# A convolution on one core: fp32 loads on SyncE with casts on ScalarE in place of casting loads on GpSimd

## The chip, the core and the metric

The kernel runs on one core of a Trainium2 chip. The metric is the device time of one execution in microseconds (us). The kernel before takes 126.02 us, the median of three runs (125.80 to 126.24).

A core has five engines with an instruction stream each: TensorE (PE in the profile, with its weight loads as PEld), VectorE (DVE), ScalarE (ACT), GpSimd (POOL) and SyncE (SP, which only issues transfers here). Sixteen DMA engines move data between HBM and the on-chip memory SBUF. SP, ACT and POOL can issue DMAs, each on a ring of its own (q1, q10 and q0 in the profile). A DMA issued by POOL may change the type on the way; here it reads fp32 and writes fp16.

## The reference: what is computed

A 3x3 convolution with padding 1: 16 images of 64 channels, 64x64 pixels, and 128 output channels, all in fp32.

```
batch, c_in, h, w, c_out = 16, 64, 64, 64, 128
x_pad = np.pad(x, ((0, 0), (0, 0), (1, 1), (1, 1)), mode='constant')
for b, co, ci, kh, kw:
    output[b, co] += weight[co, ci, kh, kw] * x_pad[b, ci, kh:kh+h, kw:kw+w]
```

The input has 16.78 MB, the output 33.55 MB.

## The kernel before

**The arithmetic.** Two output rows, 2j and 2j+1, are made together, with five products in place of six for each column kw of the filter. With w0, w1, w2 the filter's rows and s = x[2j] + x[2j+1], row 2j is w1 s + (w2 - w1) x[2j+1] + w0 x[2j-1], and row 2j+1 is w1 s + (w0 - w1) x[2j] + w2 x[2j+2]. The product w1 s is shared. The five weights lie in `Wt` as G1, G21, G0, G01 and G2; they are made at the start from `w_raw` by transposing matmuls (line 91), copies and subtractions (lines 98 to 110).

**The tiles.** The images are taken in eight pairs p = 0 to 7. Image 2p lies on partitions 0 to 63, image 2p+1 on 64 to 127, one channel to a partition. A pair has a tile `xs` of fp16 (128 x 64 x 64), a tile `ss` of the row sums s in fp16 (128 x 32 x 64), and two output tiles `ot`, one to an image (128 output channels x 64 x 64 in fp32, 16 KB to a partition).

**A pair's work.** It is cut into four blocks of 16 output rows (8 row pairs, line 144). A block is written (p, blk) below. For each, PE makes three groups of products in PSUM: U (G1 with `ss`, 6 matmuls), A (G21 and G0 with `xs`, 12 matmuls) and B (G01 and G2 with `xs`, 12 matmuls), always for both images. ACT copies U to `ut` in SBUF (line 188). DVE adds A and `ut` into the even rows of `ot` (line 196), and B and `ut` into the odd rows (line 199). PE has 30 matmuls to a block, 960 in all (line 174).

**The loads.** SP loads the weights and the pairs 0, 1 and 2 in fp32 (lines 41 to 47), into tiles of the pool that later holds the outputs. Their fp16 copies are made by casts on ACT and POOL (line 104; `later`, line 115, says at which block each piece of 16 rows is cast). The pairs 3 to 7 come by casting DMAs that POOL issues (line 60): pairs 3 and 4 at the start, pairs 5, 6 and 7 between POOL's sums in pair 1, the last two pairs in halves. These have no fp32 tile and no casts. POOL makes `ss` of the next pair in two pieces at the beginning of each pair (line 137), for pairs 1 and 2 from the fp32 tile, for the others from `xs`; DVE makes that of pair 0.

**The stores.** Pair 0's first image, and both images of pair 7, are stored in halves after blocks 1 and 3, all others whole after block 3. SP issues the stores of the first image of each pair (line 201), as soon as DVE's last add into it is done. The stores of the second image are held and issued by ACT at the next block, after that block's copies of U (line 191).

**Order.** Each engine runs its instructions in the order of the program; `keep` marks those whose order is fixed as written. A DMA waits on the engine that issues it, and then stands in that engine's ring, first in, first out. The output pool has 7 buffers, `xs` 8, `ss` 3, `ut` 4.

Of the kernel before, what the change touches and what calls it, by code (L numbers as in the profile page):

```python
# [8 lines left out]
F32 = mybir.dt.float32  # L9
F16 = mybir.dt.float16  # L10
# [3 lines left out]
def kernel(  # L14
# [6 lines left out]
    nc = tc.nc  # L21
    B, CI, H, W = x.shape
    CO = weight.shape[0]
    assert H == 64 and W == 64 and CI == 64 and CO == 128 and B % 2 == 0
    NP = B // 2
    RB = 8

    keep = tc.keep_in_program_order
    x_rows = x.rearrange("b c h w -> (b c) h w")
# [2 lines left out]

    const = ctx.enter_context(tc.tile_pool(name="const", bufs=1))
    psum = ctx.enter_context(tc.tile_pool(name="psum", bufs=8, space=bass.MemoryType.PSUM))
    xpool = ctx.enter_context(tc.tile_pool(name="xpool", bufs=8))
    opool = ctx.enter_context(tc.tile_pool(name="opool", bufs=7))
    spool = ctx.enter_context(tc.tile_pool(name="spool", bufs=3))
    upool = ctx.enter_context(tc.tile_pool(name="upool", bufs=4))

    w_raw = const.tile([CO, CI * 9], F32)  # L40
    nc.sync.dma_start(w_raw, w_flat)
    x0 = opool.tile([128, H, W], F32, tag="ot", name="x0")
    nc.sync.dma_start(x0, x_rows[0:128, :, :])
    x1 = opool.tile([128, H, W], F32, tag="ot", name="x1")
    nc.sync.dma_start(x1, x_rows[128:256, :, :])
    x2 = opool.tile([128, H, W], F32, tag="ot", name="x2")
    nc.sync.dma_start(x2, x_rows[256:384, :, :])
    raws = {1: x1, 2: x2}
    ident = const.tile([128, 128], F16)
    make_identity(nc, ident)  # L50
    w16 = const.tile([CO, CI * 9], F16)
    keep(nc.gpsimd.tensor_copy(w16, w_raw))  # L52

    xs = {p: xpool.tile([128, H, W], F16, tag="xs", name="xs") for p in range(3)}

    def load(p, rows):
        xs[p] = xpool.tile([128, H, W], F16, tag="xs", name="xs")
        for lo in range(0, H, rows):
            keep(
                nc.gpsimd.dma_start(  # L60
                    xs[p][:, lo : lo + rows, :],
                    x_rows[128 * p : 128 * p + 128, lo : lo + rows, :],
                )
            )

    ss = {}

    def sums(eng, p, src, lo, n):
        if p not in ss:
            ss[p] = spool.tile([128, H // 2, W], F16, tag="ss", name="ss")  # L70
        v = src.rearrange("p (j i) c -> p j i c", i=2)
        keep(
            eng.tensor_add(  # L73
                ss[p][:, lo : lo + n, :], v[:, lo : lo + n, 0, :], v[:, lo : lo + n, 1, :]
            )
        )
# [5 lines left out]
    def wrow(i):  # L82
        return Wt[:, i, :, :].rearrange("p t c -> p (t c)")

    wps = {}
    for kh in (1, 2, 0):
# [3 lines left out]
            for q in (0, 64):  # L90
                nc.tensor.matmul(wp[q : q + 64, k * CO : k * CO + CO], w16[:, t::9], ident)  # L91
        wps[kh] = wp[:, 0 : 3 * CO]
    blank = const.tile([128, 400], F32)
    keep(nc.vector.memset(blank, 0.0))  # L94
    warm = psum.tile([128, 512], F32, tag="acc", name="warm")
    for _ in range(3):
# [3 lines left out]
    keep(nc.vector.tensor_sub(wrow(G21), wps[2], wrow(G1)))  # L100
    keep(nc.vector.tensor_sub(wrow(G01), wps[0], wrow(G1)))  # L101

    def cast(copy, p, src, lo, hi):
        keep(copy(xs[p][:, lo:hi, :], src[:, lo:hi, :]))  # L104

    for lo in (RB, 2 * RB, 3 * RB):
        sums(nc.vector, 0, x0, lo, RB)
    cast(nc.scalar.copy, 0, x0, 0, 18)
    keep(nc.scalar.copy(wrow(G0), wps[0]))  # L109
    keep(nc.scalar.copy(wrow(G2), wps[2]))  # L110
    cast(nc.gpsimd.tensor_copy, 0, x0, 34, 50)
    cast(nc.gpsimd.tensor_copy, 0, x0, 50, 64)
    for p in (3, 4):
        load(p, H)
    later = {
        (0, 0): [(0, x0, 18, 34)],
        (0, 2): [(1, x1, 0, 16), (1, x1, 16, 32)],
        (0, 3): [(1, x1, 32, 48), (1, x1, 48, 64)],
    }
    later.update({(1, n): [(2, x2, 16 * n, 16 * n + 16)] for n in range(4)})  # L120

    held = []

    whole = {3: (0, 64)}
    halves = {1: (0, 32), 3: (32, 64)}
    cuts_of = [(halves, whole)] + [(whole, whole)] * (NP - 2) + [(halves, halves)]

    def store(eng, p, b2, ot, lo, hi):
        return eng.dma_start(
            out_rows[2 * p + b2, :, lo:hi, :],  # L130
            ot.rearrange("p j i c -> p (j i) c")[:, lo:hi, :],
        )

    for p in range(NP):
        if p + 1 < NP:
            for lo in (0, 16):
                sums(nc.gpsimd, p + 1, raws.get(p + 1, xs[p + 1]), lo, 16)
                if (p, lo) == (1, 16):
                    for q in range(5, NP):
                        load(q, H if q == 5 else H // 2)  # L140
        ots = [
            opool.tile([128, H // 2, 2, W], F32, tag="ot", name="ot") for _ in range(2)
        ]
        for blk in range(4):
            j0 = blk * RB

            def group(wi_rows):

                tiles = [
                    psum.tile([128, RB, W], F32, tag="acc", name="acc") for _ in range(2)  # L150
                ]
                n = 3 * len(wi_rows)
                i = 0
                for wi, off in wi_rows:
                    for kw in (1, 0, 2):
                        c_lo, c_hi = max(0, 1 - kw), min(W, W + 1 - kw)
                        for b2 in range(2):
                            p0 = 64 * b2
                            lo, hi = j0, j0 + RB
                            if off is None:  # L160
                                rhs = ss[p][p0 : p0 + 64, lo:hi, c_lo + kw - 1 : c_hi + kw - 1]
                            else:
                                while 2 * lo + off < 0:
                                    lo += 1
                                while 2 * (hi - 1) + off > H - 1:
                                    hi -= 1
                                first = 2 * lo + off
                                last = 2 * (hi - 1) + off
                                rhs = xs[p][
                                    p0 : p0 + 64,  # L170
                                    first : last + 1 : 2,
                                    c_lo + kw - 1 : c_hi + kw - 1,
                                ]
                            nc.tensor.matmul(  # L174
                                tiles[b2][:, lo - j0 : hi - j0, c_lo:c_hi],
                                Wt[p0 : p0 + 64, wi, kw, :],
                                rhs,
                                start=i == 0,
                                stop=i == n - 1,
                            )  # L180
                        i += 1
                return tiles

            U = group([(G1, None)])
            us = []
            for b2 in range(2):
                ut = upool.tile([128, RB, W], F32, tag="ut", name="ut")
                keep(nc.scalar.copy(ut, U[b2]))  # L188
                us.append(ut)
            while held and (p, blk) != (1, 0):  # L190
                keep(store(nc.scalar, *held.pop(0)))
            for piece in later.get((p, blk), ()):
                cast(nc.scalar.copy, *piece)
            A = group([(G21, 1), (G0, -1)])
            for b2 in range(2):
                nc.vector.tensor_add(ots[b2][:, j0 : j0 + RB, 0, :], A[b2], us[b2])  # L196
            Bt = group([(G01, 0), (G2, 2)])
            for b2 in range(2):
                nc.vector.tensor_add(ots[b2][:, j0 : j0 + RB, 1, :], Bt[b2], us[b2])  # L199
            if blk in cuts_of[p][0]:  # L200
                store(nc.sync, p, 0, ots[0], *cuts_of[p][0][blk])
            if blk in cuts_of[p][1]:
                held.append((p, 1, ots[1], *cuts_of[p][1][blk]))
    while held:
        keep(store(nc.scalar, *held.pop(0)))


# [28 lines left out]
```

## Time and profile before

| What | Value |
|---|---|
| median of the runs | 126.02 us |
| the profiled execution: its time | 126.62 us |
| its span, first to last instruction | 124.8 us |
| granted clock of PE, mean | 0.961 |
| PE busy | 108.0 us (86%), 984 matmuls |
| DVE busy | 84.5 us (68%) |
| ACT busy | 46.5 us (37%) |
| POOL busy | 38.6 us (31%) |
| bytes read from and written to HBM | 17.07 and 33.55 MB |

The profiled execution lies 1.8 us above its span. The profile has a page with the busy time of each engine, and the span in 40 slices of 3.12 us, where a digit gives the busy tenths of an engine and a line the GB/s that the DMA engines moved (counted by what they write). A table has the DMA queues with their packets, bytes and the share of the 16 engines' time. The chain that ended last is followed back from the last instruction to what released it. A group of instructions is a line of the page: the line of code, the engine, the operation, the output and the inputs with partitions x elements, the count, then the busy time in us, the mean of one in ns, and the idle time of the engine just before with what ended it. A row of the windows view is one stretch of time: its bounds, its length, then the busy us (and number of instructions) of PE, PEld, DVE, ACT and POOL, the granted clock, the DMA share and GB/s. A row of the timeline gives start and length in us, then the instruction; "SPq" and "ACTq" are the issue of a DMA on that engine. Behind the DMA rows lie records of single packets with queue, start, length and bytes.

### The profile page before, as it was taken

What the parts mean: (1) busy time and instruction counts of PE and PEld (TensorE: products, weight loads), DVE (VectorE), ACT (ScalarE), POOL (GpSimd) and SP (SyncE); (2) the same over time, 40 slices, a digit from 0 to 9 for tenths busy, and PEclk for the clock granted to TensorE, in tenths of its full rate; (3) what the DMA queues carried; (4) which work ended last, traced back from release to release, by engine and by line L of the source; (5) the groups of instructions that cost most, each with busy time, mean ns of one, the idle gap of its engine ahead of it and who ended that gap; (6) DMA issues with size and microseconds to landing.
All of it is one profiled execution on the core that took longest, in us unless ns stands there. A gap on an engine that the chain in (4) does not pass through costs nothing.

```text
span 124.8 us, 2430 instructions
## 1 busy us (share of the span) xinstructions
PE 108.0 (86%) x984; PEld 49.8 (40%) x984; DVE 84.5 (68%) x135; ACT 46.5 (37%) x78; POOL 38.6 (31%) x30
## 2 busy tenths in 40 slices
PE   0699999999999999999999999999999999990000
PEld 0544444444444444444444444444444444430000
DVE  1019987877777887888777778777877787774000
ACT  4118559966653333333333333333333333330000
POOL 2219780799975001910240032004200510000000
PEclk9999999999999999999999999999999999999555
DMA  5899999999999999999999999999999999999991
GB/s 163 367 430 451 430 302 247 278 276 312 365 344 333 341 370 385 382 392 375 370 381 386 382 400 369 354 406 400 374 369 404 425 420 430 420 420 430 428 404 68
DMA packets 4330, 45.52 MB, mean 365 GB/s; under 512 B 480, under 2 KB 480, under 8 KB 1120
## 3 DMA queue, kind: packets, MB, share of 16 engines
q1 hardware_dynamic: 2016, 23.36, 45.0%
q10 hardware_dynamic: 1296, 16.78, 31.7%
q0 software_dynamic: 1008, 5.24, 20.8%
q8 instruction: 7, 0.11, 0.3%
q14 instruction: 3, 0.02, 0.0%
HBM read 17.07 MB, written 33.55 MB: 406 GB/s over the span
## 4 chain that ended last, share of the span: by engine, by line
PE 86%; DMA 2%; DVE 1%; issue 1%; POOL 1%; DVEq 0%
PE acc L174 81%; PE warm L97 3%; DMA w_raw<-in_weight_dram 2%; PE wp L91 1%; DVE ot L196 1%; POOL w L52 1%; DVEq L231 0%; DVE ot L199 0%; DVEq L196 0%
## 5 line engine op out<-in xcount | busy, mean ns | idle before, releaser
L174 PE MATMUL acc<-xs,Wt 64*128 64x504 f16 (+3 forms) x768 | 87.0, 374 | 0.0
L174 PEld LDWEIGHTS <-Wt 64*128 64x128 f16 x960 | 46.9, 95 | 56.2 <-issue 0.9
L188 ACT COPY ut<-acc 128x512 f32<-128x512 f32 x64 | 34.4, 589 | 56.9 <-issue 39.0
L196 DVE TENSOR_TENSOR ot<-acc,ut 128x512 f32<-128x512 f32 x64 | 41.2, 685 | 20.8 <-PE acc L174 18.4
L199 DVE TENSOR_TENSOR ot<-acc,ut 128x512 f32<-128x512 f32 x64 | 41.1, 683 | 0.0
L73 POOL TENSOR_TENSOR ss<-xs 128x1024 f16<-128x1024 f16 x10 | 21.1, 2130 | 49.3 <-DMA xs<-in_x_dram 49.3
L174 PE MATMUL acc<-ss,Wt 64*128 64x504 f16 (+1 forms) x192 | 26.0, 377 | 0.0
L104 ACT CAST xs<-x 128x1024 f16<-128x1024 f32 (+1 forms) x10 | 10.5, 1070 | 3.3 <-DMA x<-in_x_dram 3.3
L73 POOL TENSOR_TENSOR ss<-x 128x1024 f16<-128x1024 f32 x4 | 9.4, 2358 | 5.0 <-DMA x<-in_x_dram 5.0
L73 DVE TENSOR_TENSOR ss<-x 128x512 f16<-128x512 f32 x4 | 3.3, 868 | 7.5 <-DMA x<-in_x_dram 7.5
L91 PE MATMUL wp<-ident,w 128*64 128x128 f16 x18 | 1.3, 328 | 4.3 <-POOL w L52 4.3
L104 POOL CAST xs<-x 128x1024 f16<-128x1024 f32 (+1 forms) x2 | 3.0, 1518 | 4.5 <-DMA x<-in_x_dram 4.5
L97 PE MATMUL warm<-blank 128*128 128x400 f32 x6 | 4.2, 864 | 0.0
L60 POOL DMA_DIRECT2D xs<-in_x_dram x7 | 3.9, 574 | 0.0
L91 PEld LDWEIGHTS <-w 128*64 128x64 f16 x18 | 1.1, 210 | 4.3 <-POOL w L52 4.3
L97 PEld LDWEIGHTS warm<-blank 128*128 128x128 f32 x6 | 1.8, 326 | 1.4 <-issue 1.3
L98 ACT CAST Wt<-wp 128x384 f16<-128x384 f32 x1 | 0.5, 478 | 3.0 <-PE wp L91 3.0
L98 ACT ACT_TABLE_LOAD x1 | 1.3, 1283 | 0.7 <-PEq L220 0.7
L52 POOL CAST w<-w_raw 128x576 f16<-128x576 f32 x1 | 0.7, 663 | 2.3 <-DMA w_raw<-in_weight_dram 2.3
L94 DVE MEMSET blank<- 128x400 f32 x1 | 0.4, 392 | 0.9 <-PEq L220 0.9
L109 ACT CAST Wt<-wp 128x384 f16<-128x384 f32 x1 | 0.5, 478 | 0.5 <-DVE Wt L101 0.5
L100 DVE TENSOR_TENSOR Wt<-wp,Wt 128x384 f16<-128x384 f32 x1 | 0.6, 551 | 0.0
(8 smaller groups left out, 1.9 us busy)
## 6 DMA issues: line engine op xcount, KB each, us to landing
out_dram<-ot ACTq DMA_DIRECT2D x7, 2048.0 KB, 19.0
out_dram<-ot SPq DMA_DIRECT2D x6, 2048.0 KB, 18.3
x<-in_x_dram SPq DMA_DIRECT2D x3, 2048.0 KB, 12.0
out_dram<-ot SPq DMA_DIRECT2D x4, 1024.0 KB, 12.6
xs<-in_x_dram POOLq DMA_DIRECT2D x3, 1024.0 KB, 22.0
xs<-in_x_dram POOLq DMA_DIRECT2D x4, 512.0 KB, 51.2
out_dram<-ot ACTq DMA_DIRECT2D x2, 1024.0 KB, 11.1
w_raw<-in_weight_dram SPq DMA_DIRECT2D x1, 288.0 KB, 2.8
```

The lines of the kernel that those rows point to most:

```text
L52: keep(nc.gpsimd.tensor_copy(w16, w_raw))
L60: nc.gpsimd.dma_start(xs[p][:, lo : lo + rows, :], x_rows[128 * p : 128 * p + 128, lo : lo + rows, :],)
L73: eng.tensor_add(ss[p][:, lo : lo + n, :], v[:, lo : lo + n, 0, :], v[:, lo : lo + n, 1, :])
L91: nc.tensor.matmul(wp[q : q + 64, k * CO : k * CO + CO], w16[:, t::9], ident)
L97: nc.tensor.matmul(warm[:, 0:400], blank[:, 0:128], blank)
L98: keep(nc.scalar.copy(wrow(G1), wps[1]))
L100: keep(nc.vector.tensor_sub(wrow(G21), wps[2], wrow(G1)))
L104: keep(copy(xs[p][:, lo:hi, :], src[:, lo:hi, :]))
L174: nc.tensor.matmul(tiles[b2][:, lo - j0 : hi - j0, c_lo:c_hi], Wt[p0 : p0 + 64, wi, kw, :], rhs, start=i == 0, stop=i == n - 1,)
L188: keep(nc.scalar.copy(ut, U[b2]))
L196: nc.vector.tensor_add(ots[b2][:, j0 : j0 + RB, 0, :], A[b2], us[b2])
L199: nc.vector.tensor_add(ots[b2][:, j0 : j0 + RB, 1, :], Bt[b2], us[b2])
```

## The change

No DMA casts any more. SP loads the pairs 0 to 4 in fp32 at the start, and then issues all stores, both images' in turn. ACT loads the pairs 5, 6 and 7 in fp32, each in two parts (rows 0 to 33, then 34 to 63), one part at the first block of each of the pairs 1 to 6 (`coming`). The fp32 tiles `raws` and the output tiles share ten buffers ("homes") that are assigned by hand (`raw_home`, `out_home`). ACT casts every pair's rows in pieces, one to a block, during the pair before; for pair 7 this begins at block (6, 1) and ends at block (7, 0). POOL makes the sums always from the fp32 tile, for pair 7 piece by piece beside the casts. Pair 0's second image is stored in halves as the first. `xs` has 3 buffers, `ss` 2, and `blank`, the zeros for three matmuls at the start, takes one of the `ut` buffers.

```diff
-    xpool = ctx.enter_context(tc.tile_pool(name="xpool", bufs=8))
-    opool = ctx.enter_context(tc.tile_pool(name="opool", bufs=7))
-    spool = ctx.enter_context(tc.tile_pool(name="spool", bufs=3))
+    xpool = ctx.enter_context(tc.tile_pool(name="xpool", bufs=3))
+    opool = ctx.enter_context(tc.tile_pool(name="opool", bufs=1))
+    spool = ctx.enter_context(tc.tile_pool(name="spool", bufs=2))
...
-    x0 = opool.tile([128, H, W], F32, tag="ot", name="x0")
-    nc.sync.dma_start(x0, x_rows[0:128, :, :])
...
+    raw_home = [0, 1, 2, 3, 4, 0, 2, 3]
+    out_home = [(5, 6), (7, 8), (9, 1), (5, 6), (7, 8), (9, 1), (4, 0), (5, 6)]
+    raws = {}
+
+    def load(eng, p, lo, hi):
+        if p not in raws:
+            raws[p] = opool.tile([128, H, W], F32, tag=f"home{raw_home[p]}", name="raw")
+        keep(
+            eng.dma_start(
+                raws[p][:, lo:hi, :], x_rows[128 * p : 128 * p + 128, lo:hi, :]
+            )
+        )
+
+    AHEAD = 5
+    for p in range(AHEAD):
+        load(nc.sync, p, 0, H)
...
-    blank = const.tile([128, 400], F32)
+    blank = upool.tile([128, 400], F32, tag="ut", name="blank")
...
-    for p in (3, 4):
-        load(p, H)
+    q4 = [(16 * n, 16 * n + 16) for n in range(4)]
     later = {
-        (0, 0): [(0, x0, 18, 34)],
-        (0, 2): [(1, x1, 0, 16), (1, x1, 16, 32)],
-        (0, 3): [(1, x1, 32, 48), (1, x1, 48, 64)],
+        (0, 0): [(0, 18, 34)],
+        (0, 2): [(1, *q4[0]), (1, *q4[1])],
+        (0, 3): [(1, *q4[2]), (1, *q4[3])],
     }
-    later.update({(1, n): [(2, x2, 16 * n, 16 * n + 16)] for n in range(4)})
-
-    held = []
+    later.update({(p, n): [(p + 1, *q4[n])] for p in range(1, NP - 2) for n in range(4)})
+
+
+    pieces = [(0, 18), (18, 34), (34, 50), (50, 64)]
+    later.update({((NP - 2) + (n + 1) // 4, (n + 1) % 4): [(NP - 1, *pieces[n])] for n in range(4)})
+    coming = {}
+    for n in range(2 * (NP - AHEAD)):
+        coming[(1 + n, 0)] = (AHEAD + n // 2, *((0, 34), (34, H))[n % 2])
...
-    cuts_of = [(halves, whole)] + [(whole, whole)] * (NP - 2) + [(halves, halves)]
+    cuts_of = [halves] + [whole] * (NP - 2) + [halves]
...
-            for lo in (0, 16):
-                sums(nc.gpsimd, p + 1, raws.get(p + 1, xs[p + 1]), lo, 16)
-                if (p, lo) == (1, 16):
-                    for q in range(5, NP):
-                        load(q, H if q == 5 else H // 2)
+            for lo in (0, 16) if p + 1 < NP - 1 else ():
+                sums(nc.gpsimd, p + 1, raws[p + 1], lo, 16)
         ots = [
-            opool.tile([128, H // 2, 2, W], F32, tag="ot", name="ot") for _ in range(2)
+            opool.tile([128, H // 2, 2, W], F32, tag=f"home{k}", name="ot")
+            for k in out_home[p]
         ]
...
-            while held and (p, blk) != (1, 0):
-                keep(store(nc.scalar, *held.pop(0)))
-            for piece in later.get((p, blk), ()):
-                cast(nc.scalar.copy, *piece)
+            if (p, blk) in coming:
+                load(nc.scalar, *coming[(p, blk)])
+            for q, lo, hi in later.get((p, blk), ()):
+                cast(nc.scalar.copy, q, lo, hi)
+                if q == NP - 1:
+                    sums(nc.gpsimd, q, raws[q], lo // 2, (hi - lo) // 2)
...
-            if blk in cuts_of[p][0]:
-                store(nc.sync, p, 0, ots[0], *cuts_of[p][0][blk])
-            if blk in cuts_of[p][1]:
-                held.append((p, 1, ots[1], *cuts_of[p][1][blk]))
-    while held:
-        keep(store(nc.scalar, *held.pop(0)))
+            if blk in cuts_of[p]:
+                for b2 in range(2):
+                    keep(store(nc.sync, p, b2, ots[b2], *cuts_of[p][blk]))
```

More of the change, by code (lines that the diff above doesn't have):

```diff
@@ L41 @@
     nc.sync.dma_start(w_raw, w_flat)
-    x0 = opool.tile([128, H, W], F32, tag="ot", name="x0")
-    nc.sync.dma_start(x0, x_rows[0:128, :, :])
[L44 to L48, printed above, removed]
+    raw_home = [0, 1, 2, 3, 4, 0, 2, 3]
[12 more added lines that the diff above has]
+        load(nc.sync, p, 0, H)
+    x0 = raws[0]
     ident = const.tile([128, 128], F16)
@@ L52 @@
     keep(nc.gpsimd.tensor_copy(w16, w_raw))
[L54 to L64, printed above, removed]
+    xs = {}
     ss = {}
@@ L101, with cast @@
     keep(nc.vector.tensor_sub(wrow(G01), wps[0], wrow(G1)))
-    def cast(copy, p, src, lo, hi):
-        keep(copy(xs[p][:, lo:hi, :], src[:, lo:hi, :]))
+    def cast(copy, p, lo, hi):
+        if p not in xs:
+            xs[p] = xpool.tile([128, H, W], F16, tag="xs", name="xs")
+        keep(copy(xs[p][:, lo:hi, :], raws[p][:, lo:hi, :]))
     for lo in (RB, 2 * RB, 3 * RB):
         sums(nc.vector, 0, x0, lo, RB)
-    cast(nc.scalar.copy, 0, x0, 0, 18)
+    cast(nc.scalar.copy, 0, 0, 18)
     keep(nc.scalar.copy(wrow(G0), wps[0]))
     keep(nc.scalar.copy(wrow(G2), wps[2]))
-    cast(nc.gpsimd.tensor_copy, 0, x0, 34, 50)
-    cast(nc.gpsimd.tensor_copy, 0, x0, 50, 64)
-    for p in (3, 4):
-        load(p, H)
+    cast(nc.gpsimd.tensor_copy, 0, 34, 50)
+    cast(nc.gpsimd.tensor_copy, 0, 50, 64)
+    q4 = [(16 * n, 16 * n + 16) for n in range(4)]
     later = {
-        (0, 0): [(0, x0, 18, 34)],
-        (0, 2): [(1, x1, 0, 16), (1, x1, 16, 32)],
-        (0, 3): [(1, x1, 32, 48), (1, x1, 48, 64)],
-    }
-    later.update({(1, n): [(2, x2, 16 * n, 16 * n + 16)] for n in range(4)})
-    held = []
+        (0, 0): [(0, 18, 34)],
+        (0, 2): [(1, *q4[0]), (1, *q4[1])],
+        (0, 3): [(1, *q4[2]), (1, *q4[3])],
+    }
+    later.update({(p, n): [(p + 1, *q4[n])] for p in range(1, NP - 2) for n in range(4)})
[4 more added lines that the diff above has]
+        coming[(1 + n, 0)] = (AHEAD + n // 2, *((0, 34), (34, H))[n % 2])
     whole = {3: (0, 64)}
     halves = {1: (0, 32), 3: (32, 64)}
-    cuts_of = [(halves, whole)] + [(whole, whole)] * (NP - 2) + [(halves, halves)]
+    cuts_of = [halves] + [whole] * (NP - 2) + [halves]
     def store(eng, p, b2, ot, lo, hi):
```

## The prediction, made before the changed kernel was run

> **What bounds the kernel now.** I read the chain that ended last first, then the page's slices, its table of DMA queues, the windows, and last the packet records behind the DMA rows. The chain, in order of time:
> ```profile
> 9.74 101.39 PE acc L174 x948
> ...
> 113.07 0.60 DVE ot L199
> ```
> By it PE never rests, 86% of the span is PE, and the last add ends at about 113.7. But the span is 124.8: eleven microseconds follow in which no engine computes. The page says what runs there:
> ```profile
> PE   0699999999999999999999999999999999990000
> ...
> DMA  5899999999999999999999999999999999999991
> ...
> q1 hardware_dynamic: 2016, 23.36, 45.0%
> q10 hardware_dynamic: 1296, 16.78, 31.7%
> q0 software_dynamic: 1008, 5.24, 20.8%
> ...
> HBM read 17.07 MB, written 33.55 MB: 406 GB/s over the span
> ```
> The DMA row is at 9 from the third slice to the last but one, and three slices longer than PE. q1 (SP), q10 (ACT) and q0 (the casting loads of POOL) add up to 97.5% of 16 engines' span. So two things are full at once: PE until 112, the DMA engines until the end; and the end belongs to DMA. The windows give its pace (columns after the engines: clock, DMA share, GB/s):
> ```profile
> 8.00:12.00 4.00, 4.00 (x27) 1.43 (x28) 3.23 (x5) 2.72 (x5) 3.19 (x3) 1.00 1.02 438
> 20.00:24.00 4.00, 4.00 (x42) 1.86 (x40) 3.27 (x6) 3.59 (x6) 1.37 (x1) 1.00 0.99 231
> 116.00:120.00 4.00, 0.00 (x0) 0.00 (x0) 0.00 (x0) 0.00 (x0) 0.00 (x0) 0.50 1.01 428
> ```
> Loads alone run at 438 GB/s (q1 alone), stores alone at 428, both at a share of 1. GB/s counts what is written, so a casting packet counts half; where casts run the figure is low without the engines being idle. I count such packets at the fp32 bytes that they read. By the packet records that makes 50.81 MB in all (23.36 + 16.78 + 2 x 5.24, the rest instructions); 0.61 MB of it is moved by 4.0 us. At 121.0 us 0.53 MB are left; the last packet ends at 123.50, since engines finish apart. The rates:
> ```
> us            MB     GB/s   what
> 4.0-15.5      4.94   429.6  fp32 loads only
> 20.0-24.0     1.46   366.2  casts at their densest, some packets 0.7 to 1.0 us
> 24.0-97.8    31.41   425.6  stores and casts
> 97.8-121.0    9.92   427.4  stores only
> 16 KB packets: q0 (8 KB written) 648 ns, median 624; q1 621 ns (stores after 24 us); 8 KB: q0 322, fp32 309
> ```
>
> **Part 1: casting loads become fp32 loads.** As many bytes are read from HBM as before, so the DMA work shrinks only by the difference in pace. At the rate without casts the mean engine is done at 4.0 + (50.81 - 0.61)/0.4274 = 121.46; now it is done at 121.0 + 0.53/0.4274 = 122.24. **Gain: 0.78 us.** Bounds: by packet means 384 x (648 - 621) + 512 x (322 - 309) ns over 16 engines = 1.06 us; if the slow stretch at 20-24 comes from something else and returns, only the 0.42% between 425.6 and 427.4 over 73.8 us stays, 0.31 us, of which instruction fetches (q8, five of its seven packets there) explain about a third: 0.2 us. I take 0.78, because the slow packets of 20-24 are nearly all on q0.
>
> **Part 2: all stores on SP's ring.** Cost 0: between 103.5 and 104.5 the packet records have q1 alone with stores (share 0.93 to 0.99 of a total of 1.01), so one ring fills 16 engines. Its issue is 0.33 us apiece on SP, which does nothing else. Each DMA completes on one of eight semaphores in turn, and the order of the built program shows each store waiting for the DMA eight places before it. Behind a waiting store stand only later stores. The nearest such wait is for a store of the pair two or three before, by my queue below landed 20 us earlier: 0.
>
> **Part 3: casts on ACT.** Five more pairs are cast there:
> ```profile
> L188 ACT COPY ut<-acc 128x512 f32<-128x512 f32 x64 | 34.4, 589 | 56.9 <-issue 39.0
> ...
> L104 ACT CAST xs<-x 128x1024 f16<-128x1024 f32 (+1 forms) x10 | 10.5, 1070 | 3.3 <-DMA x<-in_x_dram 3.3
> L73 POOL TENSOR_TENSOR ss<-x 128x1024 f16<-128x1024 f32 x4 | 9.4, 2358 | 5.0 <-DMA x<-in_x_dram 5.0
> ```
> A block lasts 3.2 us (pair 12.81, from store issues 87.49 and 100.29). ACT then has 2 x 0.59 + 1.07, and 0.4 once a pair if the issue counts: at most 2.65 us. In pair 1 before this very mix already runs and PE shows 4.00 of 4.00. Cost 0. If that cover went, each us would hit A's adds (DVE waits for `ut`), then PE. POOL's sums from fp32 take 2.36 instead of 2.13 us, twice per 12.81: 0. POOL loses seven issues of 0.57 us, on no path. `blank` and the smaller pools: their old readers are done a pair earlier (`ss`: before the block in which POOL starts; homes 5 and 6: pair 0's stores, in my queue gone at about 43, wanted again at 49): 0.
>
> **Part 4: loads come later.** Before, q0 held work in reserve until 97.8. Now ACT issues 1.11 and 0.98 MB in turn at blocks (1,0) to (6,0), so the store queue can run dry. With 0.4274 MB/us, all that was issued ahead of pair p's stores (4.19 MB a pair) is gone at: pair 1 40.2 (issue 36.3), pair 2 52.3 (49.1), pair 3 64.7 (61.9), pair 4 76.8 (74.7), pair 5 89.2 (87.5), pair 6 101.35 (100.29), pair 7's first half 111.2 (106.65), last half 116.0 (113.10). The reserve falls to **1.06 us at pair 6**. From issue to first packet:
> ```profile
> 0.74 0.38 SPq L41 DMA_DIRECT2D w_raw<-in_weight_dram  x1
> ...
> 100.29 0.33 SPq L129 DMA_DIRECT2D out_dram<-ot  x1
> ```
> The first is issued at 0.74 and has its first packet at 1.76: 1.02 us on empty engines. So the reserve just holds: 0. The other end is ACT's store issued at 26.66, whose first packet comes at 30.16, 3.50 us later, with two other rings full. I take 1.02: a ring that has run dry is the first case.
>
> **Sum.** 0.78 + 0 + 0 + 0: span 124.8 to 124.0, the profiled execution 126.62 to 125.8. That execution is 0.6 above the median of the runs, 126.02 (perhaps the slow stretch is part of that; then the gain is the small one). On the median: 126.02 - 0.78 = **125.2**. The tail between the mean engine (122.24) and the last packet (123.50) is left as it is: with no cast in flight from 97.8 on, the engines' last packets of one DMA still lay 2.2 to 3.4 us apart.
>
> **Rivals.**
> 1. *The tail shrinks too: 124.3.* The 16 completions of one DMA lay 0.58 us apart for the loads of pairs 0 and 1, before q0's first packet at 15.7; 1.6 to 2.8 us from then on. Software rings would then slow some engines, and without them the last packet would come 0.3 instead of 1.26 after the mean: 0.9 more. Against: instruction fetches hold one engine for 0.9 us each and remain; the records don't name the engine. The Trainium skill (DMA: Bandwidth & Descriptors, Latency and other measured facts) has two of 16 engines usually slower, with the software rings' port contention as its best guess. By that rule the time is this rival's; no record here shows which engines are late.
> 2. *The casts were free: 125.8.* Gain 0.2, below. For: the 0.6 between profiled execution and median. Within 0.3% (0.38 us, about what a measurement of this kernel can tell from no change).
> 3. *The queue runs dry, slower: 127.6.* If 3.50 us holds for a nearly empty ring, pair 6's stores start at 103.8; 50.81 - 42.22 = 8.59 MB are left then, 20.1 us: 123.9 instead of 122.24, +1.6. It decides from 100.29 + latency > 101.35, so from 1.06 us on, and turns the sign from 1.84 us on. Against: the 3.50 was measured behind two full rings. The Trainium skill (the same page and section) gives about 0.6 us to a hardware ring's first byte; the row has 1.02, and by either there is no idle.
> 4. *The last load comes late, slower: 127.8.* Its second part is issued at about 88.1 and its cast is due at 98.0 (cast at 33.98 in pair 1, five pairs later). At 1:2 against 16 KB packets: 0.98 MB at a third of 427 GB/s, 6.9 us, plus 1 to 3.5: 96.0 to 98.5, in time. But a 1 MB cast took 12.6 us on q0 (47.15 to 59.73), between two rings. With 3.5 + 12.6 it lands at 104.2; ACT holds the next block's copies (due 100.2) until 105.3, PE is 5 us late, the last stores go out at 118.1 instead of 113.1; they have 2.9 us of reserve less 1.0, so the mean engine ends at 118.1 + 1.0 + 2.1/0.4274 = 124.0: +1.8. That has a chance only if SP's and ACT's rings don't share evenly.
>
> **How the numbers follow.** Forecast 0.38 (its own range 124.8 to 125.6), rival 1 0.14, rival 2 0.23, rival 3 0.18, rival 4 0.07. Faster 0.38 + 0.14 = 0.52, same 0.23, slower 0.25. The range goes from rival 1 (124.2) to rival 3 (127.6), which leaves out rival 4 and a little below.
>
> **What would show it.** q0 gone from the queues, no stretch of 20-24 under 420 GB/s, PE's chain still ending near 112, last add near 113.7, a DMA row of 9 throughout with 420 to 430 GB/s in each window to 120. Wrong: GB/s under 400 for a window right after 100 (rival 3), idle time of ACT's cast on the load or PE under 4.00 near 100 (rival 4), a stretch under 400 GB/s near 20 with fp32 loads (rival 2), completions still 2 us apart but the end earlier (for the forecast and against rival 1).

## The result and the profile after

The changed kernel is slower by 1.7%: 128.11 us (median; 128.07 to 128.22) against 126.02, a ratio of 1.0167 (95% interval 1.0152 to 1.0182). The forecast was 125.2 and the range ended at 127.6. Its profiled execution took 128.11 us with a span of 126.3. That of the kernel before had been 0.6 above its median, so I traced it a second time: 126.12 us, span 124.3. Differences below are against that second trace, unless it says otherwise.

The page of the changed kernel: the slices of PE and of DMA, then the queues.
```profile
PE   0499999999999999999999999999999999960000
...
DMA  5999999999999999999999999999999999999960
...
q1 hardware_dynamic: 3744, 44.34, 83.5%
q10 hardware_dynamic: 864, 6.29, 12.2%
```
q0 is gone, PE is at 9 as long as before, and the DMA row is at 9 without a hole: nothing ran dry and nobody stalled. The chain of waits says the same of the compute:
```profile
9.71 101.61 PE acc L180 x948
...
113.27 0.60 DVE ot L207
```
The last add ends at 113.9, 0.2 later than before. So the two microseconds come after the compute, among the stores that are left. The windows (engines, then clock, DMA share, GB/s):
```profile
24.00:28.00 4.00, 4.00 (x40) 1.84 (x38) 2.73 (x5) 2.85 (x6) 1.14 (x1) 1.00 1.01 375
28.00:32.00 4.00, 4.00 (x40) 1.86 (x38) 3.21 (x6) 2.77 (x4) 0.00 (x0) 1.00 0.97 371
...
120.00:124.00 4.00, 0.00 (x0) 0.00 (x0) 0.00 (x0) 0.00 (x0) 0.00 (x0) 0.50 0.54 227
124.00:128.00 4.00, 0.00 (x0) 0.00 (x0) 0.00 (x0) 0.00 (x0) 0.00 (x0) 0.50 0.01 6
```
and of the second trace of the kernel before:
```profile
120.00:124.00 4.00, 0.00 (x0) 0.00 (x0) 0.00 (x0) 0.00 (x0) 0.00 (x0) 0.50 0.50 209
124.00:128.00 4.00, 0.00 (x0) 0.00 (x0) 0.00 (x0) 0.00 (x0) 0.00 (x0) 0.71 0.00 0
```
From 120 to 124 the sixteen engines do nearly the same work (shares 0.54 and 0.50, a difference of 0.16 us). But the changed kernel has a share of 0.01 after 124: one engine that is still at work while fifteen have ended. The 16 completions of the very last DMA show it, in us after the first of them:
```
before    121.56 + 0 .1 .1 .2 .3 .5 .5 .8 1.1 1.4 1.5 1.6 1.6 1.7 1.7 1.8
changed   121.52 + 0 .. seven within 0.4, eight from 1.4 to 2.1, and one at 4.0
```
The mean engine (from the packet records, the engines busy at each moment from 115 us on) ends at 122.39 instead of 122.15, and the last packet at 125.05 instead of 123.04. **So 0.24 us of the loss is the mean engine, and 1.77 us is the tail between it and the last packet, which grew from 0.89 to 2.66.** Together 2.01; the medians differ by 2.09.

How the lone engine falls behind can be followed in the packet records. They don't name an engine, but a packet starts where its engine's one before ended, and so they can be sorted into sixteen chains. From 35 us on, in the changed kernel (q8 is the queue of TensorE's instruction fetches):
```
chains ending at      q8 fetches (start, us)           packets longer than usual
121.2-121.6, seven    none                             one of 113 ns, one of 107 ns
122.6-123.3, eight    46.6 59.1 73.5 86.7 101.0        behind a fetch 0.36 to 0.46 us each, few others
125.05, one           none                             none over 100 ns, but 3.83 us in all
```
TensorE's instruction fetches explain most of the middle group: one takes 0.88 to 0.96 us of one engine and its next packet some 0.4 us more. With the two before 35 us (at 19.2 and 32.1) there are seven of them, for eight chains. The last chain is another matter. It has many packets that are a little long: 16 KB take mostly 626 to 660 ns instead of 611. These excesses sum to 3.83 us between 35 and 114 us, 4.8% of that time and about its lag of 4.0 us; the other fifteen chains have next to none of them. Where two chains run in step the sorting can swap them, but the count of such packets says the same: with stores alone, from 104 to 112 us, 15 packets are a little long, about as many as one engine moves in 8 us. After 114, when the compute is over, the excesses are 4 ns in all. I call this the **slow engine**, and the sum of all excesses of 3 to 99 ns over the usual duration of a packet of that queue and size (leaving out an excess of exactly 13 ns, the usual one beside a casting packet: 624 ns for 16 KB, 322 for 8 KB) the **small excess**. Per 6 us, in ns:
```
from us          28  34  40  46  52  58  64  70  76  82  88  94 100 106 112
before, again     0   6  21  99   0  46  28   0   0   0   0 117 380 326  52
changed         464 328 212 352 208 324 262 338 239 340 295 270 331 369  73
```
In the kernel before it is there too, but from about 97 us only, just where the last casting packets leave q0; in the changed one it runs from the first stores to the end of the compute. That is the **slow-engine theory**: one DMA engine moves packets some 5% slower while TensorE works and stores run, except while casting packets are in flight. Removing the casts uncovers it for some 85 instead of 16 us. (Number 7 shows that "while TensorE works" was put too narrowly.)

### The profile page after: what moved, and what is told of

Same layout as the page of the kernel before. It is cut to its first block, busy times and chain, and to the rows that moved or that the text cites. A ratio compares the mean times of both kernels' runs of the same rounds, so it can differ in the third digit from the quotient of the medians.

```text
span 126.3 us, 2458 instructions
## 1 busy us (share of the span) xinstructions
PE 107.5 (85%) x984; PEld 49.8 (39%) x984; DVE 84.5 (67%) x135; ACT 65.4 (52%) x98; POOL 37.5 (30%) x25
## 4 chain that ended last, share of the span: by engine, by line
PE 80%; DMA 6%; DVE 2%; issue 1%; DVEq 0%; SPq 0%
PE acc L180 80%; DMA raw<-in_x_dram 6%; DVE ot L204 1%; DVE ss L75 1%; DVEq L236 0%; DVE ot L207 0%; SPq L41 0%; DVEq L204 0%
## 5 line engine op out<-in xcount | busy, mean ns | idle before, releaser
L75 POOL TENSOR_TENSOR ss<-raw 128x1024 f16<-128x1024 f32 (+3 forms) x16 | 33.1, 2092 | 56.7 <-DMA raw<-in_x_dram 22.3
L108 ACT CAST xs<-raw 128x1024 f16<-128x1024 f32 (+2 forms) x30 | 31.6, 1062 | 4.1 <-DMA raw<-in_x_dram 4.1
L75 DVE TENSOR_TENSOR ss<-raw 128x512 f16<-128x512 f32 x4 | 3.3, 867 | 7.7 <-DMA raw<-in_x_dram 7.7
L108 POOL CAST xs<-raw 128x1024 f16<-128x1024 f32 (+1 forms) x2 | 3.0, 1519 | 4.2 <-DMA raw<-in_x_dram 4.2
L99 PE MATMUL warm<-blank 128*128 128x400 f32 x6 | 3.4, 733 | 0.0
L100 ACT CAST Wt<-wp 128x384 f16<-128x384 f32 x1 | 0.5, 478 | 3.4 <-PE wp L93 3.4
L113 ACT CAST Wt<-wp 128x384 f16<-128x384 f32 x1 | 0.5, 478 | 0.5 <-DVE Wt L103 0.5
L114 ACT CAST Wt<-wp 128x384 f16<-128x384 f32 x1 | 0.5, 485 | 0.0
## 6 DMA issues: line engine op xcount, KB each, us to landing
raw<-in_x_dram ACTq DMA_DIRECT2D x3, 1088.0 KB, 12.1
raw<-in_x_dram ACTq DMA_DIRECT2D x3, 960.0 KB, 11.8
```

The lines of the kernel that those rows point to most:

```text
L75: eng.tensor_add(ss[p][:, lo : lo + n, :], v[:, lo : lo + n, 0, :], v[:, lo : lo + n, 1, :])
L99: nc.tensor.matmul(warm[:, 0:400], blank[:, 0:128], blank)
L100: keep(nc.scalar.copy(wrow(G1), wps[1]))
L108: keep(copy(xs[p][:, lo:hi, :], raws[p][:, lo:hi, :]))
```

## The experiments

Four kernels were run first, before I had seen this pattern. The three theories in their expectations are about the way the stores are split over rings (ring), TensorE's instruction fetches of 16 KB on single engines (fetch), and the late fp32 loads (load).

**1. The second images' stores back on ACT.** Changed kernel with
```
+                keep(store(nc.scalar, *held.pop(0)))
...
-                for b2 in range(2):
-                    keep(store(nc.sync, p, b2, ots[b2], *cuts_of[p][blk]))
+                keep(store(nc.sync, p, 0, ots[0], *cuts_of[p][blk]))
+                held.append((p, 1, ots[1], *cuts_of[p][blk]))
+    while held:
+        keep(store(nc.scalar, *held.pop(0)))
```


> The changed kernel, but the stores of the second images are issued by ACT at the next block, as the kernel before does; loads, casts and sums stay as changed. In the changed kernel 15 DMA engines finish their last packets between 121.5 and 123.7 and one at 125.5. Ring theory (one ring for all stores lets one engine fall behind): the late engine is gone, its last completion lies at most 2.5 us after the first, time 126.3 to 126.8. Fetch theory (the late engine is the one that moved more instructions for TensorE, whatever the rings): unchanged, 127.8 to 128.4. Load theory (the fp32 loads, with their slow stretch at 25 to 29 us and their parts on ACT's ring, make it late): also unchanged.

Measured: 128.86 us, ratio 1.0237 (1.0173 to 1.0301). The slices, and the issues of the late loads (median us from issue to landing):
```profile
PE   0599999999999999999999999999999990999500
...
DMA  5999999999999999999999999999999999969595
...
raw<-in_x_dram ACTq DMA_DIRECT2D x3, 960.0 KB, 20.2
```
The loads now queue behind stores on their own ring and land 20.2 us after their issue (11.8 in the changed kernel). The last one comes too late, ACT waits with a cast, PE stops for a slice, and all 16 last completions lie within 0.13 us, by 125.5. This is my rival 4, produced by the experiment. It says nothing of the tail, because the engines ran dry ahead of the last stores and started them together; but it shows what that rival costs, and that it isn't what happened in the changed kernel, whose PE row has no hole.

**2. Part 2 alone: the kernel before with all stores on SP.**
```
-            while held and (p, blk) != (1, 0):
-                keep(store(nc.scalar, *held.pop(0)))
...
-                held.append((p, 1, ots[1], *cuts_of[p][1][blk]))
+                keep(store(nc.sync, p, 1, ots[1], *cuts_of[p][1][blk]))
```


> The kernel before with its casting loads, but all stores issued by SP, both images in turn. Ring theory: slower by 1.4 to 2.1 us, 127.4 to 128.1, one engine 3.5 us or more behind the first. Fetch theory: within 0.5 of the kernel before, if the fetches fall on the engines as there; load theory: within 0.4 of it, since nothing of the loads is changed.

Measured: 126.73 us, ratio 1.0058 (1.0041 to 1.0075). So Part 2 costs something by itself, some 0.7 us, where I had put 0. With one store ring instead of two, the casting loads are through sooner: q0's last packets end at 72 us instead of, by engine, 92 to 98. In the windows (DMA share and GB/s at the end) around 72:
```profile
68.00:72.00 4.00, 4.00 (x40) 1.83 (x38) 3.27 (x6) 1.34 (x3) 0.18 (x1) 1.00 1.03 406
72.00:76.00 4.00, 4.00 (x42) 1.88 (x40) 2.81 (x5) 1.88 (x4) 4.00 (x2) 1.00 1.00 422
```
The small excess is 0 to 111 ns per 6 us from 28 to 70 us and 262, 324, 368, 332, 330, 340, 347 after it. It was in this run that I saw the switch. The last completions show a single engine behind it: the last of the sixteen came 1.7 us after the first for the DMA that ended at 98 us, then 1.9, 2.2 and 2.4 for those at 103, 108 and 113, while the others stayed within 1.7. A second thing to see is the share: 1.03 with casts, 1.00 without. More than 1 means that packets overlap in the records.

**3. The six late load parts on SP instead of ACT** (`load(nc.sync, ...)`).

> The changed kernel, but the six late parts of the loads are issued by SP too, right behind the stores of the pair before: a single ring for everything. Load theory in its part on the rings (packets of two rings mixed on an engine): spread of the last completions back to 2.5 us, time about 126.7. Ring theory: unchanged or worse, 128 to 128.5. Fetch theory: unchanged, 127.8 to 128.4.

Measured: 128.13 us, ratio 1.0167 (1.0150 to 1.0183): the time of the changed kernel, by another way. Its waits from 96 us on:
```profile
ACT xs L108 <- DMA raw<-in_x_dram: 7.1, 1, 7.1
...
PE acc L180 <- ACT ut L194: 3.5, 1, 3.5
```
A load behind stores on SP's ring lands 17.1 us after its issue, ACT waits 7.1 us for it and PE 3.5 us for ACT; the last completions lie within 0.4 us. Equal times here are a coincidence; only the trace tells the two apart.

**4. Two thirds of the matmuls: the odd rows take A's sums** (`Bt = A`).

> The changed kernel without the third group of products (12 of 30 matmuls of a block): the odd rows get the second group's sums again, so the output is not the convolution; loads, casts, additions and stores stay. TensorE then needs 40% fewer instructions and 4 or 5 fetches in place of 7, and leaves the DMA engines the only bound. Fetch theory: the late engine is gone, the last completions lie 2 us apart, and the end comes 2 us earlier or more, about 126 or less. Ring theory: the spread stays at 3.5 to 4 us and the time at 127.5 to 128.2.

Measured: 126.73 us, ratio 1.0069 (1.0041 to 1.0098), with the fp32 loads, the casts on ACT and every store of the changed kernel in place; the third group of products is left out. Small excess between 34 and 112 us: 2.41 us instead of 3.87. TensorE's fetches went from 7 to 4 as well, so fetch and slow engine were not yet told apart.

The second batch tested the slow engine.

**5. The kernel before, again.**

> The kernel before, unchanged: a second trace of it, since its first profiled execution took 0.6 us more than its median. Expected 126.0 us. Slow-engine theory (one DMA engine moves 16 KB store packets 15 to 45 ns slower than the other fifteen as long as the compute engines work, and this shows only while the software ring of the casting loads is empty; the kernel before shows it from 94 to 112 us only, the changed one from 28 to 113): the small excesses over 611 ns sum to about 2 us, all of them after 90 us, and the last DMA's completions lie within 2.5 us of one another without a lone late one. Fetch theory (the end is set by which engines took TensorE's instruction fetches): the last engine is one that had a fetch late. If the excess runs from 28 us on here too, the slow-engine theory falls.

Measured: 126.10 us. The row "before, again" above is this run: no excess to speak of until 94 us. That execution and the first one differ by 0.5 us, and so do their last packets (123.04 and 123.51), with the small excess between 34 and 112 us at 1.02 and 1.47 us.

**6. The late parts from GpSimd, still in fp32** (`load(nc.gpsimd, ...)`): a software ring without a cast.

> The changed kernel with its six late load parts issued by GpSimd, still fp32, so that a software ring is in flight without a cast. Slow-engine theory, if any packets of a software ring hide the slowness: small excesses near 0 while the ring has packets (until about 90 us), sum 2 instead of 4.7 us, time 126.0 to 126.8. Slow-engine theory, if it takes casting packets: as the changed kernel, 128.1. Ring theory (software rings are what makes an engine late): 128.1 or more, the lone last engine later than 4.0 us after the first.

Measured: 128.58 us, ratio 1.0177 (1.0124 to 1.0230).
```profile
DMA  5999999999999999999999999999999999999970
...
q1 hardware_dynamic: 3744, 44.34, 83.6%
q0 software_dynamic: 864, 6.29, 12.2%
```
q0 is back with the same bytes as q10 in the changed kernel, and it hides nothing: 270 to 540 ns per 6 us from 34 us on, 4.42 us between 34 and 112. Sorted into chains from 45 us on, most of it (3.29 us by one sorting) lies on one engine again, which ends at 125.15 (another, late since earlier, ends with it). So it isn't the software ring but the cast that hides the slow engine.

**7. 800 tiny memsets on GpSimd**, 25 a block.

> The changed kernel with 800 one-column memsets on GpSimd, 25 a block, some 40% more instructions in all and no work to speak of. If the slow engine is slowed by something done once per instruction: the sum of the excesses goes from 4.7 to about 6.5 us, the time to 129.5. If by the work of the matmuls or by anything else that goes with time: 128.1, sum 4.7.

Measured: 173.06 us. The experiment failed by its own weight. The line of the memsets, and a wait:
```profile
L192 POOL MEMSET tick<- 128x1 f32 x800 | 78.6, 98 | 45.7
...
PE acc L181 <- POOL ss L76: 22.7, 5, 7.2
```
98 ns apiece were enough to make POOL's sums late, and PE waited for them. So the time says nothing of the slow engine. But one of these waits of PE does, because stores fill the DMA engines meanwhile:
```profile
50.00:54.00 4.00, 0.00 (x0) 0.00 (x0) 0.79 (x2) 0.00 (x0) 2.51 (x26) 1.00 0.99 422
54.00:57.00 3.00, 0.41 (x4) 0.15 (x5) 0.00 (x0) 0.00 (x0) 2.94 (x4) 0.50 1.01 431
```
From 50 to 54 us PE has no matmul, DVE ends two adds, and POOL runs the memsets: the small excess is 220 ns, as much as in the changed kernel with PE at full work (200 in the same stretch). At 54.2 the memsets end and POOL turns to two long sums: until 57 the excess is 0, with POOL busy throughout. **So the slowness doesn't need TensorE: in this stretch it goes with POOL's many short instructions, and stops when they stop.** It is also gone where compute waits in other runs while stores go on: the excess is 0 from 104 to 106 us in number 1 and from 104 to 105.4 in number 3 (a wait for a load), and 4 and 8 ns from 44 to 48 us in numbers 4 and 8 (a wait for an output buffer).

**8. One fifth of the matmuls: group U alone.**
```
-            A = group([(G21, 1), (G0, -1)])
+            A = U
...
-            Bt = group([(G01, 0), (G2, 2)])
+            Bt = A
```


> The changed kernel with group U alone, 6 of a block's 30 matmuls (even and odd rows are both U + U, so it isn't the convolution); loads, casts, sums, adds and stores are all there. Compute then ends near 96 instead of 113 us. If the slow engine's slowness goes with the matmuls: excesses of some 60 instead of 280 ns in 6 us, sum about 1 us, no lone late engine, time about 125.0. If it goes with time in which engines compute: 280 ns in 6 us until 96, sum 3.6, time about 126.9. Fetch theory: with two TensorE fetches or fewer no engine is late and the time is about 125.0 even if the excesses stay.

Measured: 126.19 us, ratio 0.9991 (0.9953 to 1.0029).
```profile
PE   0695466788788803879888288783170000000000
...
PEclk9999995555555555555555555555555555555555
```
```profile
92.00:96.00 4.00, 0.03 (x1) 0.00 (x0) 4.00 (x7) 1.89 (x4) 0.00 (x0) 0.50 1.01 434
...
120.00:124.00 4.00, 0.00 (x0) 0.00 (x0) 0.00 (x0) 0.00 (x0) 0.00 (x0) 0.50 0.37 158
124.00:128.00 4.00, 0.00 (x0) 0.00 (x0) 0.00 (x0) 0.00 (x0) 0.00 (x0) 0.76 0.00 0
```
DVE, ACT and the DMAs do all of their work until past 92 us, but PE has a fifth of its matmuls (they take longer apiece at the lower clock, so its row is still filled). From 34 to 94 us the small excess sums to 1.11 us, against 2.90 in the changed kernel, and by the chains it makes no engine late any more: the three that end last have next to none of it (from 45 us on). On how many of the others it lies, the sorting doesn't settle. The last completions lie within 1.5 us, and nothing runs after 124. So the excess falls with the matmuls, if not in proportion, and doesn't go with compute time at large. It comes nearer to a proportion with the instructions of all engines, as the windows view counts them: from 34 to 94 us there are 1272 in the changed kernel, 863 in number 4 and 396 here, which is 2.3, 2.5 and 2.8 ns of excess for each (the memsets of number 7 made some 8 each, so the count alone isn't the whole rule). I had set 125.0 us for that; this profiled execution took 125.64, the median is 0.55 more. With so little excess, the changed kernel's traffic has, by the median, the time of the kernel before; not all of the gain need be the slow engine's, since the mean engine ends earlier too (121.64 instead of 122.39). (Fetches fell from 7 to 1 here as well; numbers 2 and 9, with all 7, are what shows that fetches alone don't make the tail.)

**9. Casts, spread like the changed kernel's loads.** The kernel of number 2, with the casting loads of pairs 5 to 7 in halves, one at the start of each pair from 1 to 6:
```
-                    for q in range(5, NP):
-                        load(q, H if q == 5 else H // 2)
...
+            if blk == 0 and 1 <= p <= 6:
+                load(5 + (p - 1) // 2, 32, [32 * ((p - 1) % 2)])
```
(`spool` has 2 buffers here, and the last sum of pair 7 stands behind its load.)

> The kernel before with all stores on SP and the casting loads of pairs 5 to 7 issued in halves, one half a pair from pair 1 to pair 6, the places where the changed kernel issues its fp32 parts. Each half is 8 packets an engine, which beside 16 KB stores take some 7.5 of a pair's 12.8 us: casting packets are in flight for about 60% of the time from 30 to 100 us, with gaps. Slow-engine theory, by casts: the small excesses come and go with the casting packets: near 0 in the stretches that have them, 40 to 60 ns a us in the gaps, the sum 2 to 3 us (4.0 with all stores on SP and casts until 72, 4.9 with fp32 loads from the software ring); time 126.3 to 126.9. If what hides the slowness is something else than casting packets (the depth of the queues, the number of rings, the first 72 us): no such pattern, excess either throughout or after 72 us only.

Measured: 126.37 us, ratio 1.0025 (0.9988 to 1.0061). This is the twin of number 6: the same two rings, late loads at about the same places, cast or not (pairs 3 and 4 are cast here too).
```profile
q1 hardware_dynamic: 3312, 40.14, 76.7%
q0 software_dynamic: 1152, 5.24, 20.9%
```
In steps of 2 us from 38 on, the casting packets that start, and the small excess of the others in ns:
```
us       38  40  42  44  46  48  50  52  54  56  58  60  62  64  66  68  70  72  74  76  78  80
casting   1   5  33  34  44  12   0   0  31  34  38  25   0   0  13  35  38  41   1   0   0   0
excess   60 101   0   0   0   0  87 120  26   0   0   0  70 157  70   0   0   0   9 121  92  99
```
The slowness goes off when casting packets come and on again when they are gone, gap by gap. Over 28 to 112 us, the 24 steps with at least 8 casting packets have 17 ns each, the 13 with none 100 ns. The hiding isn't without exception: the step at 98 us, where casting packets set in again, has 38 of them and 194 ns. Number 6's last packet comes 1.66 us later than this one's: 0.86 us of that is tail (the small excess is 4.42 against 2.09 us), 0.80 a mean engine that ends later, for which I have no experiment.

**10. The same in twice as many, smaller DMAs**, to have casts in flight all the time (`load(..., 16, [lo, lo + 16])`).

> The same with each half in two DMAs of 16 rows: 16 smaller packets an engine, which by turns with 16 KB stores take about 12 of a pair's 12.8 us, so casting packets are in flight nearly always from 30 to 105 us. Slow-engine theory, by casts: excesses near 0 until about 103 us, sum under 1.2 us, last completions within 2 us; time 125.7 to 126.2, at or just under the kernel before. Otherwise: 126.5 or more with an excess that runs on under the casts, or a mean engine that ends later by the price of twice as many packets.

Measured: 128.30 us, ratio 1.0187 (1.0118 to 1.0257). The hiding worked as expected: casting packets in every step from 28 to 78 us, and an excess of exactly 0 for the other packets in all of them. The time didn't, for a reason of its own: the small packets queue for longer, POOL's sums wait for them and issue the next loads late, and the last sum holds PE:
```profile
PE   0699999999999999999999999999999993399400
```
```profile
POOL ss L74 <- DMA xs<-in_x_dram: 19.7, 2, 10.1
...
PE acc L177 <- POOL ss L74: 4.3, 1, 4.3
```

The kernels whose DMA engines had work without a break up to the last stores, ordered by the small excess (us; the tail is the last packet less the mean engine):
```
                          excess 34-112  mean engine  last packet  tail  this execution  median
5 before, again                1.02        122.15       123.04     0.89      126.12      126.10
8 one fifth of matmuls         1.16        121.64       122.70     1.06      125.64      126.19
before, first trace            1.47        122.27       123.51     1.24      126.62      126.02
9 casts spread                 2.09        122.23       123.50     1.27      126.70      126.37
4 two thirds of matmuls        2.41        122.03       123.64     1.61      126.66      126.73
2 all stores on SP             2.45        122.16       123.51     1.35      126.72      126.73
changed kernel                 3.87        122.39       125.05     2.66      128.11      128.11
6 fp32 from GpSimd             4.42        123.03       125.16     2.13      128.67      128.58
```
The mean engine hardly moves but in 6 and 8; the tail, and with it the time, grows with the excess, if not line by line (fetches and single late packets add to both). No version here beats the kernel before, and none was in sight: its typical execution already has as little excess as one with a fifth of the matmuls.

## Why the prediction was wrong, point by point

**The step that failed** is the sentence after the sum: "The tail between the mean engine (122.24) and the last packet (123.50) is left as it is". It grew by 1.77 us. I had the sixteen completions in hand and reasoned that they were just as uneven when no cast was in flight (97.8 on). What I didn't ask is *when* the unevenness had been made. The slow engine collects its lag as long as stores run without casts beside computing engines: 16 us of that in the kernel before, some 85 in the changed one. The spreads of single DMAs were a poor guide besides, and misread: by the trace's completions they lay 2.2 to 4.5 us apart from 97.8 on, not 2.2 to 3.4, and in rival 1 they were 0.53 for the first loads and 1.0 to 5.8 after, not 0.58 and 1.6 to 2.8. A spread that adds up over time can't be read off at the end of one kernel and carried to another.

**Part 1, gain 0.78: came out as a loss of 0.24 on the mean engine.** The packets did get cheaper as I had counted: the sum of all their durations over 16 engines fell from 122.30 to 121.57, by 0.73. But the durations are no cost where they overlap. From 4 to 114 us the kernel before had 1.80 us more packet time than time (shares of 1.01 to 1.03 with casts), the changed one 0.85. The difference of 0.95 takes the gain back, and 0.95 - 0.73 = 0.22 is the loss. Nor were the slow packets of 20 to 24 us the casts': the same stretch, 366 GB/s then, is in the changed kernel at 24 to 32 us with 375 and 371 GB/s and no cast at all. Between 18 and 34 us, packets over 100 ns late cost 0.91 us of the mean engine, and 0.61 in the kernel before. In every run such a stretch sits where the first stores start. That was the condition of my rival 2, with a chance of 0.23 and "the casts were free"; by the mean engine they were rather better than free.

**Part 2, cost 0: 0.7 us** by number 2. One ring did fill 16 engines, as the row had it, and no store waited. The cost came by a way that I hadn't looked for: with one store ring fewer, q0 is done sooner, and the slow engine is uncovered for 40 us instead of 16.

**Part 3, cost 0: right.** ACT casts all pairs and PE's chain is 101.61 us long, against 101.39.

**Part 4, cost 0: right.** The reserve held at 100.49, where pair 6's stores are issued: the DMA row has 9 throughout. The loads landed 11.8 to 12.1 us after their issue, and from 30 us on ACT's casts waited once, 1.1 us, for one.

**Rival 1 had the right place and the wrong sign.** It said that software rings make some engines late, so that the tail would shrink without them. The Trainium skill (DMA: Bandwidth & Descriptors, Latency and other measured facts) gives two of 16 engines as usually slower and takes software rings for the best guess, as something specific to them. Here the late engine is there with hardware rings alone (4.0 us after the first), 3.3 us with a software ring in fp32, and, but for the exception in number 9, gone while casting packets are in flight; these runs speak against that guess for this kernel, if the engine that is late here is one of those two, which the records don't tell. **Rivals 3 and 4** gave times near the truth (127.6 and 127.8) for things that didn't happen; numbers 1 and 3 show how rival 4 looks when it does.

**What stays open:** why one engine is slow while instructions run (the profile takes a record of each, and no run here tells the instructions from their records), why loads alone don't show it (8 ns from 10 to 22 us in the changed kernel, with PE busy from 9.71), and why a casting packet among the others hides it. The records name no engine, so whether it is the same one in each run isn't known either. That it is one engine in the changed kernel rests on the last completions and on the sorted chains; that it goes with instructions, TensorE's being most of them, rests on numbers 4 and 8, which also have a lower clock at times and fewer fetches, and on one stretch of 7 us in number 7.

## What to carry to other kernels

Where DMA sets the end, the end is the slowest of sixteen engines and not the mean one: look at the sixteen completions of the last DMA and of some earlier ones, and ask since when the late one has been falling behind, and what in the traffic mix would change that. A packet's recorded duration is a cost only as far as packets don't overlap (a DMA share above 1 says that they do). And a slow stretch belongs to a kind of packet only if it goes away with it; that two things stood at the same place in one trace doesn't show it.

## What the runs showed of the hardware that was not expected

- One DMA engine moved 16 KB packets in 626 to 660 ns instead of 611, 4.8% of its time, while the engines computed and stores ran, and in 611 as soon as the compute was over or stood still. Memsets alone kept it up with TensorE idle (220 ns of excess in 4 us), long sums alone did not (0 in 3 us). With casting packets in flight there was 17 ns of such excess in 2 us, without 100.
- Each of TensorE's seven instruction fetches (q8, 16 KB, 0.88 to 0.96 us) fell on one DMA engine and made that one end about 1.3 us later than the engines without.
- With two store rings and q0 the casts were in flight until 92 to 98 us, with one store ring until 72.
- A load of about 1 MB on a ring of its own landed 11.8 us after its issue; behind stores on ACT's ring 20.2, on SP's 17.1.
